# First mixer of a decoder trunk: reversed value rows through DRAM, and a head's diagonal blocks masked in one operation

## Chip, cores and metric

The kernel runs on one core of a Trainium2 chip. The metric is the device time of one execution in microseconds (us), and the median of several runs is compared. In the text, PE is TensorE (matmuls), DVE is VectorE, ACT is ScalarE, POOL is GpSimd and SP is SyncE, which here only issues transfers.

## What is computed

Two consecutive layers of a decoder, on 256 tokens of width 2048 in fp32. Layer 0 mixes with a gated MLP over chunks (A) and a gated linear recurrence, HGRN2 (B); layer 1 mixes with forgetting attention; behind each mixer stands a gated MLP with a short convolution. The change concerns mixer B of layer 0 alone. Cut to what matters:

```python
def hgrn2(q, f_logit, i, g, lower_bound, o_gain):     # (1, 256, 8 heads x 128)
    log_f = logaddexp(log(lb), log1p(-lb) + log_sigmoid(fl))
    k = (1.0 - lb) * sigmoid(-fl)
    ...
    def step(state, xs):                               # chunks of 64 tokens
        G = cumsum(lf_c, axis=2)
        o_inter = einsum('bhtk,bhkv->bhtv', q_c * exp(G), state)
        decay = exp(where(mask[:, :, None], G_t - G_s, -inf))
        scores = einsum('bhtk,bhtsk,bhsk->bhts', q_c, decay, k_c)
        o_intra = einsum('bhts,bhsv->bhtv', scores, v_c)
        ...
    o = rms_norm(o, o_gain) * silu(g)

def mixer_ab(h, ...):
    u, v, q, f, i, g = split(h @ w_in, cuts, axis=-1)   # i are the values of B
    ...
    return concatenate([y_a, hgrn2(q, f, i, g, ...)], axis=-1) @ w_out
```

## The kernel before

**Projections.** The weights stream from DRAM in pieces of 128 x 1024 floats. SP issues the loads, ACT makes the high half of each piece (`wh`, L182), DVE the low half (`wl`, L183), and PE multiplies three times: high by high, high by low, low by high. Three pairs of `wh` and `wl` are kept in the first mixer. `project` gives one head's columns of the query (L301, 24 matmuls for a piece), `project_four` four blocks at a time (L344 to L346), and `project_tok` rows by tokens (L325 to L327), which is what the values use.

**Order of the work.** The tiles and the semaphores are made by a framework that orders each engine's instructions when the program is built: by the place in the program, and by when their operands are expected to be ready. The author steers it by generators. `tick()` is called once for each piece of weights and moves each generator in flight on to its next `yield`; `depth` says how many may be in flight; `held` puts an instruction behind the latest `wh` or `wl`, and `tied` puts a matmul behind the latest matmul of the projection. `start` runs a generator up to its first `yield` at once.

**The heads.** `hgrn(h)` is one generator per head, for eight heads, each begun at least four ticks (`PACE`) after the one before. The 256 tokens of a head lie as two halves of 128, and the second half (T = 1) is kept in reverse order. Step by step:

1. Factors: ACT and DVE make `lf` and `kd` (L695, L699), POOL multiplies (L701 to L709).
2. Diagonal blocks: 16 small matmuls (L714, 32 x 32 each) into a PSUM bank `dg`; four DVE operations (L717) multiply the blocks by the mask `two` into the head's square `st`.
3. Levels: products for spans of 1 to 64 tokens; DVE multiplies factors into `kq` (L722, L733, L736), ACT copies pieces to `E` (L729).
4. Five ticks later, matmuls of the levels (L743, L751) go to a bank `xps` and two tiles of PSUM kept for the purpose, `within[0]` (four levels) and `within[1]` (the level of one token's span, columns 0 to 127). ACT copies from `xps` (L754, L756), and DVE copies five levels into `st` under a mask (L762, `copy_predicated`); ACT then reverses a half to `s1` (L765).
5. Five or six ticks later, and not before the values of its four heads are there (`itoks`), the head's output: L773 to L775, then ACT (L777, L781).

**The values.** `values(j)` runs ahead of the query projections of heads 4 and 7 and makes the values of four heads each. The second half must have its rows reversed. For this `project_tok` is given a place `room`, and POOL copies each piece of the activations in reversed order (`ar`, L316), so that the products of T = 1 come out reversed. The factors of the rows (`Rt`) are reversed too, once, by `mirror` (seven small DVE operations, L616 to L621), to `Rr`. Two ACT operations (L798) take the products from PSUM to `itok`.

The order of the stages in the first mixer is: values of A, forget gates, queries of heads 0 to 3, values 0, queries 4 to 6, values 1, query 7, gates of B, `u` of A, output projection.

Of the kernel before, what the change touches and what calls it, by code (L numbers as in the profile page):

```python
# [8 lines left out]
F32 = mybir.dt.float32  # L9
F32R = mybir.dt.float32r  # L10
U16 = mybir.dt.uint16
AF = mybir.ActivationFunctionType
ALU = mybir.AluOpType
AX = mybir.AxisListType

P = 128
S = 256
# [7 lines left out]
BLK = 32  # L25
# [8 lines left out]
LANE = 64  # L34
SMALL = 4
LEVELS = (64, 32, 16, 8, 4, 2, 1)
NL = len(LEVELS)
# [17 lines left out]
def tile_trunk(ctx: ExitStack, tc: tile.TileContext, x, pp_d, cst_d, mlev_d, msk_d,  # L55
               w_v, w_f, w_g, w_i, w_q, w_u, w_abo, w_cf, w_cqkv, w_cg, w_co, w_up, w_dn, spw_d, spb_d, out):
    nc = tc.nc
    V, SC, PE = nc.vector, nc.scalar, nc.tensor
# [9 lines left out]
    def nm(base):  # L68
        count[0] += 1
        return f"{base}_{count[0]}"  # L70
# [3 lines left out]
    for c0, n in ((0, 1), (1, 1), (2, 2), (4, 2), (6, 2), (8, 4), (12, 4)):  # L74
        t = cp.tile([P, n, S], F32, tag=f"x{c0}", name=f"x{c0}")
# [29 lines left out]
    def view(ap, off, *dims):  # L105
        return bass.AP(ap.tensor, ap.offset + off, [list(ap.ap[0])] + [list(d) for d in dims])
# [12 lines left out]
    def bank():  # L119
        return psum["pool"].tile([P, 512], F32, tag="px", name=nm("px"), bufs=psum["banks"])  # L120
# [21 lines left out]
    def start(g):  # L142

        if next(g, g) is not g:
            flight.append(g)
# [64 lines left out]
    def cols2(ap):  # L210
        return ap.rearrange("p (b c) -> p b c", b=2)
# [4 lines left out]
    def of_two(ps):  # L216
        return view(ps, 0, (1, 2), (2, 256))
# [89 lines left out]
    def project_tok(wsrc, norm, room=None):  # L307

        ps = [pm.tile([P, 512], F32, tag="pm", name=nm("pm")) for _ in range(2)]
        for k in range(0, KT, 2):  # L310
            tick()
            wh, wl = weights(wsrc[:, k * 512:(k + 2) * 512], 1024)
            if room is not None:
                ar = room()
                for i in range(2):
                    nc.gpsimd.tensor_copy(ar[:, i * S:(i + 1) * S].rearrange("p (u n) -> p u n", u=2),  # L316
                                          view(norm.a[k + i], S - 1, (S, 2), (-1, P)))
            for T in range(2):
                for i in range(2):
                    a = norm.a[k + i]  # L320
                    ah, al = a[:, T * P:(T + 1) * P], a[:, S + T * P:S + (T + 1) * P]
                    if T and room is not None:
                        ah, al = ar[:, i * S:i * S + P], ar[:, i * S + P:(i + 1) * S]
                    h, l = (by_two(t, i) for t in (wh, wl))
                    PE.matmul(to_two(ps[T]), ah, h, start=k + i == 0, stop=False)  # L325
                    PE.matmul(to_two(ps[T]), ah, l, start=False, stop=False)  # L326
                    deep["last"] = PE.matmul(to_two(ps[T]), al, h, start=False, stop=k + i == KT - 1)  # L327
        return ps
# [59 lines left out]
    def held(r, last="wh"):  # L388

        tc.add_manual_dep(r.ins, deep[last].ins.name, order, reason="not before")  # L390
# [98 lines left out]
    def mixer_ab(norm):  # L489
        es = ExitStack()  # L490
        hp = es.enter_context(tc.tile_pool(name="hp", bufs=1))
        px = banks(es, 2)
# [18 lines left out]
        for g, ps in enumerate(project_first(w_v, norm, lambda: queue.append(finish()))):  # L511
# [5 lines left out]
            else:  # L517
                drain()
                Rt = norm.Rt
# [20 lines left out]
        two = hp.tile([P, 2, P], F32, tag="pairs", name="pairs")  # L540
# [9 lines left out]
        def tied(r):  # L550
            tc.add_manual_dep(r.ins, deep["last"].ins.name, order, reason="not before")
            return r
# [15 lines left out]
        def mixes():  # L568
            def sums(g, T):
                i = (2 * g + T) * 4  # L570
                j = hp.tile([P, 512], F32, tag="junk", name=nm("junk"), bufs=1)
                held(V.tensor_tensor(j, gv[g][:, T], gv[g][:, T], ALU.mult), "wl")
                V.tensor_reduce(ss[:, i:i + 4], j.rearrange("p (h d) -> p h d", d=P), AX.X, ALU.add)

            halves_ = [(g, T) for g in (1, 0) for T in range(2)]
            for i, (g, T) in enumerate(halves_):
                yield
                held(act(cols2(gv[g][:, T]), of_two(last[T]) if g else cols2(gv[0][:, T]), AF.Gelu,
                         scale=Rt[:, T:T + 1]))
                if i:  # L580
                    sums(*halves_[i - 1])
            yield
            sums(*halves_[-1])
            yield
            tables()
            rsq(ss[:, 0:2 * NH], ss[:, 0:2 * NH], P)
            bound()
            for g in range(2):
                yield
                for T in range(2):  # L590
                    i = (2 * g + T) * 4
                    v4 = gv[g][:, T].rearrange("p (h d) -> p h d", d=P)
                    held(V.tensor_tensor(v4, v4, ss[:, i:i + 4].unsqueeze(2).to_broadcast([P, 4, P]),
                                         ALU.mult), "wl")
            yield
            held(V.tensor_tensor(wt[0], wt[0], tri.unsqueeze(1).to_broadcast([P, NH, P]), ALU.mult), "wl")
            yield
            yield
            for h in range(0, NH, 2):
                ps = bank()  # L600
                both = [mix(h + i, ps[:, i * S:(i + 1) * S]) for i in range(2)]
                for m in both:
                    next(m)
                for m in both:
                    next(m, None)
                yield
            yield from mirror()


        Rr = hp.tile([P, LANE], F32, tag="Rr", name="Rr")[:, 0:2]  # L610

        def mirror():
            yield
            r = hp.tile([P, 512], F32, tag="junk", name=nm("junk"), bufs=1)
            ra, rb = (r[:, i * BLK:(i + 1) * BLK] for i in range(2))
            held(V.tensor_copy(ra, Rt[:, 1:2].to_broadcast([P, BLK])), "wl")  # L616
            V.tensor_copy(Rr[:, 0:1], Rt[:, 0:1])
            V.transpose(rb, ra)
            V.transpose(ra, view(rb, BLK - 1, (-1, BLK)))
            for a in range(4):  # L620
                V.tensor_copy(Rr[BLK * (3 - a):BLK * (4 - a), 1:2], ra[BLK * a:BLK * (a + 1), 0:1])  # L621


        gam = pp[:, C_GAM:C_GAM + 3 * NH]
# [38 lines left out]
        for j in range(2):  # L663
            ps = project_four(w_f[4 * j:4 * j + 4], A, KT)
# [3 lines left out]
            t = hp.tile([P, 1024], F32, tag="o", name=nm("turn"), bufs=2)  # L668
# [5 lines left out]
        itoks, left, os_ = [], [NH], []  # L674
# [5 lines left out]
        for st in sts:  # L680
            V.memset(st, 0.0)

        within = [px.tile([P, 512], F32, tag=f"lv{i}", name=f"lv{i}") for i in range(2)]
        for w in within:
            V.memset(w, 0.0)
        first = [0]
# [1 line left out]
        def hgrn(h):  # L688
# [19 lines left out]
                tot[2 * n] = tots[:, S - 2 * m:S - m]  # L708
                nc.gpsimd.tensor_tensor(tot[2 * n], view(tot[n], 0, (2, m)), view(tot[n], 1, (2, m)), ALU.mult)  # L709
            yield  # L710
            dg = bank()
            for T in range(2):
                for r in range(0, P, BLK):
                    tied(PE.matmul(dg[r:r + BLK, T * BLK:(T + 1) * BLK], kd[:, T, r:r + BLK], t[:, 2 - T, r:r + BLK],  # L714
                                   start=True, stop=True))
            for r in range(0, P, BLK):
                V.tensor_tensor(st[r:r + BLK, :, r:r + BLK], dg[r:r + BLK, 0:2 * BLK].rearrange("p (a b) -> p a b", a=2),  # L717
                                two[r:r + BLK, :, r:r + BLK], ALU.mult)
            yield

            qs = view(t, 2 * P, (1 - P, 2), (2, H))
# [32 lines left out]
            SC.activation(back(s128), xps[:, 0:P], AF.Copy)  # L754
            for r in (0, H):
                SC.activation(st[r:r + H, r // H, H - r:P - r], xps[r:r + H, P:P + H], AF.Copy)  # L756
            for li in reversed(range(1, NL - 1)):

                n = LEVELS[li]
                d, c = places[li]  # L760
                sv = view(st[:, 1], 0, (2 * n, 64 // n), (n - P, 2), (1, n))
                V.copy_predicated(sv, *(t_.rearrange("p (b two n) -> p b two n", two=2, n=n)  # L762
                                        for t_ in (msk[:, li * P:(li + 1) * P], d[:, c:c + P])))
# [27 lines left out]

        gz = []

        def values(j):
            ps = project_tok(w_i[j], norm, lambda: hp.tile([P, 512], F32R, tag="ar", name=nm("ar"), bufs=3))
            itok = hp.tile([P, 2, 512], F32, tag="tok", name=nm("itok"), bufs=2)
            for T in range(2):
                SC.activation(cols2(itok[:, T]), of_two(ps[T]), AF.Copy, scale=Rr[:, T:T + 1])  # L798
            itoks.append((itok, steps[0]))

        silu = []

        def gated(j):
            while left[0] > NH - 4 * (j + 1):
# [23 lines left out]

        for h in range(NH):
            if h in (4, 7):  # L830
                values(len(itoks))
            while len(kq) <= h:
                tick()
            if h % 4 == 0:
                os_.append(hp.tile([P, 2, 512], F32, tag="o", name=nm("o"), bufs=2))
            ps = project(w_q[h], A)
            for T in range(2):
                q = kq[h][:, 2 - T]
                SC.activation(back(q) if T else q, view(ps, T, (2, P)), AF.Copy, scale=omlb[:, h:h + 1])
            queue.append(hgrn(h))  # L840
# [591 lines left out]
```

## Time and profile before

| what | before |
|---|---|
| median of 3 runs | 2175.03 us (2174.26 to 2176.19) |
| the profiled execution | 2173.92 us |
| its span | 2172.1 us |
| granted TensorE clock | 1.00 |
| busy: PE, DVE, ACT, POOL | 2164.0, 1601.1, 1313.6, 472.3 us |
| matmuls | 10874 |
| DMA traffic | 483.55 MB, mean 223 GB/s |

The span is the time from the first to the last instruction of the profiled execution. "Busy" adds up the time in which an engine executes; matmuls overlap each other, and their ends are modelled. The rows of groups give the line of the kernel, the engine, the operation, output and input by the program's names, the shapes, the count, then busy time in us, the mean duration in ns, and the idle time of the engine before these instructions with what ended it. The rows of waits give the total in us, how often, and the longest. The rows of a timeline begin with the start and the length in us.

### The profile page before, as it was taken

How to read it: one execution, taken by the hardware profiler on the slowest of the kernel's cores; microseconds unless marked ns; L12 is line 12 of the kernel's file. 1: busy time of each engine (PE TensorE's matmuls, PEld its weight loads, DVE VectorE, ACT ScalarE, POOL GpSimd, SP SyncE). 2: the span in 40 equal slices, each digit the busy share in tenths (PEclk: the TensorE clock that was granted, in tenths of full speed). 3: DMA queues.
4: the chain of work that ended last, by engine and by line, in shares of the span. 5: the costliest groups of instructions: out<-in, count | busy, mean ns of one | idle time of the engine just before them, and what ended most of it. 6: DMA issues, size and time to landing. Idle time of an engine off the chain costs nothing.

```text
span 2172.1 us, 32509 instructions
## 1 busy us (share of the span) xinstructions
PE 2164.0 (100%) x10874; PEld 1900.8 (88%) x10874; DVE 1601.1 (74%) x2286; ACT 1313.6 (60%) x1951; POOL 472.3 (22%) x865
## 2 busy tenths in 40 slices
PE   9999999999999999999999999999999999999999
PEld 8988888888888888888888888888888888888888
DVE  7788768777567757776987887877777577667766
ACT  7678766665556545654666556666666466456642
POOL 1252221212012002111233443212211012011202
PEclk9999999999999999999999999999999999999999
DMA  8655677777676767776777766787777677666866
GB/s 311 209 160 177 209 238 222 240 233 236 210 228 206 235 209 219 226 237 206 241 230 229 238 207 209 221 246 222 230 227 242 198 232 217 228 215 204 251 212 192
DMA packets 492617, 483.55 MB, mean 223 GB/s; under 512 B 115137, under 2 KB 460369, under 8 KB 492321
## 3 DMA queue, kind: packets, MB, share of 16 engines
q1 hardware_dynamic: 465888, 453.27, 66.2%
q0 software_dynamic: 24832, 25.92, 5.1%
q10 hardware_dynamic: 1728, 2.28, 0.3%
q8 instruction: 85, 1.39, 0.3%
q14 instruction: 84, 0.68, 0.1%
HBM read 435.18 MB, written 2.11 MB: 201 GB/s over the span
## 4 chain that ended last, share of the span: by engine, by line
PE 94%; DVE 2%; ACT 2%; issue 1%; DMA 1%; POOL 0%; SPq 0%; ACTq 0%; DVEq 0%
PE pm L344 26%; PE pm L345 26%; PE pm L346 26%; PE pm L325 4%; PE pm L326 4%; PE pm L327 4%; PE pm L233 1%; PE pm L301 1%; ACT wh L182 1%; DVE wl L183 1%; DMA pt<-ptmp 1%; PE pm L257 1%; DVE kq L733 0%; ACT E L729 0%; DVE st L762 0%
## 5 line engine op out<-in xcount | busy, mean ns | idle before, releaser
L183 DVE TENSOR_TENSOR wl<-w,wh 128x1024 fp32r<-128x1024 f32 (+1 forms) x820 | 990.9, 1218 | 448.7 <-ACT wh L182 437.0
L182 ACT ACTIVATE wh<-w 128x1024 fp32r<-128x1024 f32 (+1 forms) x820 | 856.0, 1049 | 608.8 <-PE pm L346 447.7
L344 PE MATMUL pm<-wh,a 128*128 128x512 f32 x1728 | 655.9, 380 | 0.0
L345 PE MATMUL pm<-wl,a 128*128 128x512 f32 x1728 | 655.3, 379 | 0.3 <-DVE wl L183 0.3
L346 PE MATMUL pm<-wh,a 128*128 128x512 f32 x1728 | 654.9, 379 | 0.0
L364 POOL DMA_DIRECT2D zt<-tmp x413 | 223.5, 549 | 1134.6 <-DVE tmp L357 1022.6
L345 PEld LDWEIGHTS pm<-wl,a 128*128 128x128 f32 x1728 | 326.6, 189 | 47.4 <-DVE wl L183 1.4
L346 PEld LDWEIGHTS pm<-wh,a 128*128 128x128 f32 x1728 | 326.6, 189 | 46.2
L344 PEld LDWEIGHTS pm<-wh,a 128*128 128x128 f32 x1728 | 326.5, 189 | 46.2
L344 PE MATMUL pm<-wh,hid 128*128 128x512 f32 x688 | 260.8, 379 | 0.0
L345 PE MATMUL pm<-wl,hid 128*128 128x512 f32 x688 | 260.8, 379 | 0.0
L346 PE MATMUL pm<-wh,hid 128*128 128x512 f32 x688 | 260.8, 379 | 0.0
L326 PE MATMUL pm<-wl,a 128*128 128x512 f32 x416 | 158.1, 380 | 2.3 <-DVE wl L183 2.3
L325 PE MATMUL pm<-wh,a 128*128 128x512 f32 x416 | 158.7, 381 | 0.0
L327 PE MATMUL pm<-wh,a 128*128 128x512 f32 x416 | 157.8, 379 | 0.0
L345 PEld LDWEIGHTS pm<-wl,hid 128*128 128x128 f32 x688 | 130.0, 189 | 18.5
L346 PEld LDWEIGHTS pm<-wh,hid 128*128 128x128 f32 x688 | 130.0, 189 | 18.5
L344 PEld LDWEIGHTS pm<-wh,hid 128*128 128x128 f32 x688 | 130.0, 189 | 18.4
L1238 ACT ACTIVATE conv<-zt,pp 128x256 f32<-128x256 f32 x176 | 95.9, 590 | 70.6 <-DMA zt<-tmp 62.5
L364 POOL DMA_DIRECT2D turn<-tmp x160 | 86.9, 551 | 224.4 <-DVE tmp L357 129.6
L1239 DVE SCALAR_TENSOR_TENSOR conv<-zt,pp,conv 128x255 f32<-128x255 f32 x176 | 80.2, 479 | 54.4 <-ACT conv L1238 35.4
L357 DVE STREAM_TRANSPOSE tmp<-z 128x512 f32<-128x512 f32 x120 | 97.8, 851 | 7.1 <-ACT z L1224 5.1
(252 smaller groups left out, 2245.2 us busy)
## 6 DMA issues: line engine op xcount, KB each, us to landing
w<-in_w_up SPq DMA_DIRECT2D x352, 512.0 KB, 5.0
w<-in_w_dn SPq DMA_DIRECT2D x176, 512.0 KB, 5.0
w<-in_w_cqkv SPq DMA_DIRECT2D x96, 512.0 KB, 4.6
w<-in_w_abo SPq DMA_DIRECT2D x32, 512.0 KB, 4.9
w<-in_w_cg SPq DMA_DIRECT2D x32, 512.0 KB, 5.3
w<-in_w_co SPq DMA_DIRECT2D x32, 512.0 KB, 4.9
zt<-tmp SPq DMA_DIRECT2D x414, 32.0 KB, 2.6
zt<-tmp POOLq DMA_DIRECT2D x413, 32.0 KB, 2.4
```

Of the source, the lines that this page charges most:

```text
L182: r = deep["wh"] = SC.activation(wh, w, AF.Copy)
L183: deep["wl"] = V.tensor_tensor(wl, w, wh.bitcast(F32), ALU.subtract)
L325: PE.matmul(to_two(ps[T]), ah, h, start=k + i == 0, stop=False)
L326: PE.matmul(to_two(ps[T]), ah, l, start=False, stop=False)
L327: deep["last"] = PE.matmul(to_two(ps[T]), al, h, start=False, stop=k + i == KT - 1)
L344: PE.matmul(to_rows(ps[T]), ah, h, start=not begun and k + i == ks[0], stop=False)
L345: PE.matmul(to_rows(ps[T]), ah, l, start=False, stop=False)
L346: deep["mm"] = deep["last"] = PE.matmul(to_rows(ps[T]), al, h, start=False, stop=not more and k + i == ks[-1] + 1)
L357: V.transpose(tmp.rearrange("p (b m i t) -> p b m i t", b=4, m=4, t=2)[:, :, :, :, T], src(T).rearrange("p (m b j) -> p b m j", m=4, b=4))
L364: queues[(a + b) % len(queues)].dma_start(dst[BLK * b:BLK * (b + 1), :, a * n:(a + 1) * n], tmp[BLK * a:BLK * (a + 1), b * 4 * n:(b + 1) * ...
L1238: held(SC.activation(c, z, AF.Identity, bias=pp[:, cb:cb + 1], scale=w(2)))
L1239: V.scalar_tensor_tensor(c[:, 1:], z[:, :S - 1], w(1), c[:, 1:], ALU.mult, ALU.add)
```

## The change

The values: `project_tok` is called without `room`, so POOL copies nothing, and the products of T = 1 come out in normal order. ACT takes them to a tile `late`, with the unreversed factors `Rt`. A new generator `flip` then moves `late` to DRAM, from there to DRAM with the rows reversed, and from there to `itok[:, 1]`: three transfers of 256 KB, all issued on ACT's queue, with a tick between them. The values are entered in `itoks` with the third, two ticks later than before. `mirror` and `Rr` go.

The diagonal blocks: the 16 matmuls write into columns 128 to 383 of `within[1]`, each block in its own place in two 128 x 128 fields, which were set to zero once. One DVE operation multiplies the whole field by `two` into the whole of `st`. The bank `dg` is no longer taken. In the level copies, level 1 (a span of 32) moves from the last place to the first.

```diff
-            yield from mirror()
-
-        Rr = hp.tile([P, LANE], F32, tag="Rr", name="Rr")[:, 0:2]
-
-        def mirror():
...
-        within = [px.tile([P, 512], F32, tag=f"lv{i}", name=f"lv{i}") for i in range(2)]
+        within = [px.tile([P, n], F32, tag=f"lv{i}", name=f"lv{i}") for i, n in enumerate((512, 512))]
...
-            dg = bank()
+            dg = within[1][:, P:3 * P].rearrange("p (a b) -> p a b", a=2)
             for T in range(2):
                 for r in range(0, P, BLK):
-                    tied(PE.matmul(dg[r:r + BLK, T * BLK:(T + 1) * BLK], kd[:, T, r:r + BLK], t[:, 2 - T, r:r + BLK],
+                    tied(PE.matmul(dg[r:r + BLK, T, r:r + BLK], kd[:, T, r:r + BLK], t[:, 2 - T, r:r + BLK],
                                    start=True, stop=True))
-            for r in range(0, P, BLK):
-                V.tensor_tensor(st[r:r + BLK, :, r:r + BLK], dg[r:r + BLK, 0:2 * BLK].rearrange("p (a b) -> p a b", a=2),
-                                two[r:r + BLK, :, r:r + BLK], ALU.mult)
+            V.tensor_tensor(st, dg, two, ALU.mult)
...
-            for li in reversed(range(1, NL - 1)):
+            for li in (1, *reversed(range(2, NL - 1))):
...
+        def flip(itok, late, r, f):
+            SC.dma_start(r, late)
+            yield
+            SC.dma_start(bass.AP(f.tensor, f.offset, [[S, 2], [512, P], [1, S]]),
+                         bass.AP(r.tensor, r.offset + (P - 1) * 512, [[S, 2], [-512, P], [1, S]]))
+            yield
+            SC.dma_start(itok[:, 1], f)
+            itoks.append((itok, steps[0]))
+
         def values(j):
-            ps = project_tok(w_i[j], norm, lambda: hp.tile([P, 512], F32R, tag="ar", name=nm("ar"), bufs=3))
+            ps = project_tok(w_i[j], norm)
             itok = hp.tile([P, 2, 512], F32, tag="tok", name=nm("itok"), bufs=2)
-            for T in range(2):
-                SC.activation(cols2(itok[:, T]), of_two(ps[T]), AF.Copy, scale=Rr[:, T:T + 1])
-            itoks.append((itok, steps[0]))
+            late = hp.tile([P, 512], F32, tag="ar", name=nm("late"), bufs=1)
+            SC.activation(cols2(late), of_two(ps[1]), AF.Copy, scale=Rt[:, 1:2])
+            SC.activation(cols2(itok[:, 0]), of_two(ps[0]), AF.Copy, scale=Rt[:, 0:1])
+            start(flip(itok, late, *rowsd[j]))
...
+        dp = es.enter_context(tc.tile_pool(name="da", bufs=1, space=bass.MemoryType.DRAM))
+        rowsd = [[dp.tile([P, 512], F32, tag=f"rd{i}{n}", name=f"rd{i}{n}") for n in range(2)] for i in range(2)]
...
-                values(len(itoks))
+                values(h // 7)
```

More of the change, by code (lines that the diff above doesn't have):

```diff
@@ L606, in mixes @@
                 yield
-            yield from mirror()
-        Rr = hp.tile([P, LANE], F32, tag="Rr", name="Rr")[:, 0:2]
-        def mirror():
[L613 to L621, printed above, removed]
         gam = pp[:, C_GAM:C_GAM + 3 * NH]
```

## Prediction

> **What bounds the kernel now.** I read the page first.
>
> ```profile
> span 2172.1 us, 32509 instructions
> PE 2164.0 (100%) x10874; PEld 1900.8 (88%) x10874; DVE 1601.1 (74%) x2286; ACT 1313.6 (60%) x1951; POOL 472.3 (22%) x865
> ```
>
> TensorE (PE) is busy for 2164.0 of 2172.1 us, and the change adds and removes no matmul: 16 block products per head stay 16 products, and a projection with reversed stationary rows stays a projection. So the time can fall only by PE's idle time. The second view is the waits of PE alone:
>
> ```profile
> PE pm L326 <- DVE wl L183: 2.3, 3, 1.3
> PE warm L149 <- DVE ones L85: 1.1, 1, 1.1
> PE pm L301 <- DVE wl L183: 0.6, 1, 0.6
> PE pm L345 <- DVE wl L183: 0.3, 1, 0.3
> ```
>
> These are all that PE waits for in the whole span, 4.3 us; the warm-up's 1.1 is out of reach, so 3.2 us remain. All three of them wait for `wl`, the low half of a weight piece that VectorE (DVE) makes. L326 is the token projection that the values use. The third view, stretches of 10 us (sum, then busy time and count of PE, weight loads, DVE, ACT and POOL; clock, DMA share, GB/s), shows that the waits lie where the change is made:
>
> ```profile
> 122.00:132.00 10.00, 9.92 (x107) 8.33 (x105) 8.52 (x19) 6.31 (x18) 7.70 (x13) 1.00 0.59 189
> 132.00:142.00 10.00, 8.38 (x105) 7.21 (x106) 8.61 (x13) 7.24 (x19) 9.64 (x15) 1.00 0.51 157
> 182.00:192.00 10.00, 9.42 (x116) 8.75 (x115) 8.08 (x18) 8.47 (x27) 0.94 (x3) 1.00 0.43 135
> ```
>
> The clock is 1.00. PE drops to 8.38 of 10 where DVE is at 8.61 and GpSimd (POOL) at 9.64. Fourth, the chain of waits between 128 and 140 us (start, length, what):
>
> ```profile
> 130.27 0.23 DVE st L717
> 130.53 0.45 DVE st L762
> 132.05 1.11 DVE wl L183
> 135.09 1.34 DVE wl L183
> 136.47 0.48 PE pm L326
> ```
>
> Here the path runs over DVE: the masks of a head's diagonal blocks (L717), the copies of its levels (L762), then the `wl` for which PE waits. DVE work taken out of this place can come back as PE time, up to the 3.2 us.
>
> **Part 1: one mask operation for four.** DVE in the stage of the heads (out<-in, count, busy, mean ns, idle):
>
> ```profile
> L183 DVE TENSOR_TENSOR wl<-w,wh 128x1024 fp32r<-128x1024 f32 x25 | 31.4, 1258 | 4.3 <-ACT wh L182 4.2
> L733 DVE TENSOR_TENSOR kq<-kq,tot 128x256 f32<-128x256 f32 x31 | 16.1, 519 | 7.5 <-ACT E L729 7.5
> L717 DVE TENSOR_TENSOR st<-px,pairs 32x64 f32<-32x64 f32 x24 | 5.3, 221 | 0.4
> ```
>
> Four masks cost 4 x 0.221 = 0.884 us a head. The new one is 128x256 with one operand in PSUM, a form that the trace doesn't have. Above: 0.519, the same shape at L733. Below: 1.258 / 4 = 0.31 from L183, which does four times the columns. I take 0.45, nearer to L733. Saved: 0.43 us a head, 3.5 us in eight heads (2.9 to 4.6), all on DVE and none of it directly on PE.
>
> **Part 2: no POOL copies.** 32 casts of 128x256 go:
>
> ```profile
> L316 POOL CAST ar<-a x32: 395/586/1447, 5.6 to 178.0; 128x256 fp32r<-128x256 f32 x32
> 124.44 4.49 POOL L316 CAST ar<-a 128x256 fp32r<-128x256 f32 x6
> 126.03 1.41 DVE L183 TENSOR_TENSOR wl<-w,wh 128x1024 fp32r<-128x1024 f32 x1
> 127.37 0.61 DVE L733 TENSOR_TENSOR kq<-kq,tot 128x256 f32<-128x256 f32 x1
> 178.63 1.23 DVE L183 TENSOR_TENSOR wl<-w,wh 128x1024 fp32r<-128x1024 f32 x1 [0.31 <-ACT wh L182]
> 179.78 0.42 DVE L733 TENSOR_TENSOR kq<-kq,tot 128x256 f32<-128x256 f32 x1
> ```
>
> PE waited for none of the casts, so their own time is hidden behind PE's work. But six of them stand from 124.44 to 128.93, and the DVE operations inside that stretch took 1.41 and 0.61 us where the same operations took 1.23 and 0.42 without them: 0.2 us each. With some three such operations under the casts before each of the waits, that is 0.6 us of DVE for the first values stage and about as much for the second. [...]
>
> Reversing the rows' factors (`mirror`) goes too:
>
> ```profile
> L621 DVE COPY Rr<-junk 32x1 f32<-32x1 f32 x4 | 0.6, 145 | 0.1
> ```
>
> Seven operations of about that size, some 1 us of DVE (seven by 145 ns), all before the heads begin, where PE has no wait in the list. Worth nothing.
>
> Together: of the three waits on `wl`, 2.9 us fall in the values stages or at their end. The longest is 1.3 us, with one mask right ahead of it and casts shortly before. I let 2.0 of the 3.2 us go (0 to 3.2). What is late next is the ScalarE (ACT) cast `wh`, ahead of each `wl` (the 4.2 us of idle in the L183 row).
>
> **Part 3: the diagonal products get another place.** Before, they went to a bank of their own; now they go to columns 128 to 383 of the PSUM tile whose columns 0 to 127 hold the last level of an earlier head. The order in time at present:
>
> ```profile
> 125.51 0.53 PE L751 MATMUL lv<-E 128*32 128x32 f32 x38
> 125.99 0.33 PE L714 MATMUL px<-kq,kd 128*32 128x32 f32 x16
> 129.93 0.43 ACT L756 ACTIVATE st<-px 64x64 f32<-64x64 f32 x2
> 130.53 0.45 DVE L762 COPY_PREDICATED st<-msk,lv 128x128 f32<-128x128 uint16 x1
> 131.02 0.30 DVE L762 COPY_PREDICATED st<-msk,lv 128x128 f32<-128x128 uint16 x1
> 141.73 0.51 ACT L729 ACTIVATE E<-kq 128x128 f32<-128x128 f32 x2
> 151.62 0.39 PE L743 MATMUL px<-kq 128*128 128x128 f32 x2
> ```
>
> Head 0's levels (L751) are followed at once by head 2's diagonal products (L714, 0.33 us for 16), and DVE copies head 0's levels only 4.5 us later. The new list of levels puts level 1 first, so the copy out of the shared tile is the second, ending at 131.3. If the products must wait for it, they stand 131.3 - 126.0 = 5.3 us later; behind them are VectorE's `kq` product (L722), which overwrites what they read, and that head's twelve copies to `E` (L729). The last of these ends at 142.2, and PE takes up that head's levels only at 151.6 (L743), so 5 us there are covered by the 9.4 us between. What isn't covered is PE itself, which takes its instructions in order. Price per head, for the six heads that have a predecessor by two: 0 if the build puts other matmuls ahead of the products, 5.3 us if it doesn't. That it orders by expected readiness is seen in this trace: the first casts of L316 run at 5.6 us, though they belong to the values stage. What is left is its error of expectation, whose nearest row is PE's own longest wait on DVE, 1.3 us, in a list where most pieces have none. I take 0.25 us a head, +1.5 us in all, and keep 0 to 5.3.
>
> [...]
>
> **Part 4: the second half of the values goes through DRAM.** Out by one transfer, reversed by a second, in by a third, each waiting for the one before, all issued on ACT's queue, in two stages. Rows for the cost (KB and us to landing; the ACT queue's issue in ns):
>
> ```profile
> w<-in_w_i SPq DMA_DIRECT2D x16, 512.0 KB, 3.6
> turn<-tmp SPq DMA_DIRECT2D x8, 32.0 KB, 2.5
> L524 ACTq DMA_DIRECT2D kst<-in_msk x1: 659/659/659, 40.8 to 40.8; - x1
> DMA to landing us min/median/max: 3.1/6.2/8.2
> ```
>
> A transfer of 256 KB lies between 2.5 and 8.2 us, nearest to the 3.6 of a 512 KB piece in the same stage; three make 7.5 to 24.6, taken as 10.8. When the values are needed:
>
> ```profile
> 140.32 1.26 ACT L798 ACTIVATE itok<-pm,Rr 128x512 f32<-128x512 f32 x2
> 145.59 0.39 PE L773 MATMUL px<-itok,st 128*128 128x128 f32 x2
> 185.24 5.40 PE pm L301 x46
> 186.65 0.67 ACT L798 ACTIVATE itok<-pm,Rr 128x512 f32<-128x512 f32 x1
> 196.72 0.38 PE L773 MATMUL px<-itok,st 128*128 128x128 f32 x2
> ```
>
> Head 0's output (L773) begins 4.0 us after the values are in SBUF; the code moves it on by one piece of weights, 24 matmuls, 24/46 x 5.40 = 2.8 us. At 10.8 us the values come 10.8 - 6.8 = 4.0 us after that place. Head 4's output has 9.4 us: 1.4 late. Again PE loses this only where it reaches the product too early; the third transfer is known to the build as a long step, so other matmuls can stand ahead. I take a quarter of 5.4 us, rounded down: +1.0 us (0 to 5.4).
>
> On ACT each stage gains three issues of 0.33 to 0.66 us and two waits for a landing. Queued behind such a wait are the `wh` casts of the next pieces, and DVE and PE behind those. ACT works 6.3 to 8.5 of 10 us in this stage, so six issues, 2 to 4 us, mostly fit into its idle time: +0.5 us (0 to 3).
>
> **Sum.** On the profiled execution (2173.92 us for a span of 2172.1): -2.0 + 1.5 + 1.0 + 0.5 = +1.0, so 2174.9. The median of the runs, 2175.03, lies 1.1 higher: 2176.0 us. About 0.2%, 4.35 us, is what a measurement of this kernel can tell from no change, so this counts as no change.
>
> **The rivals.**
>
> *PE waits at the diagonal products.* One mechanism: the products sit in PE's order right behind the levels or too soon after, and wait for DVE's second level copy. For it: they stand next to each other now, and DVE is 4.5 us behind at that place. Against it: the order is made by expected readiness, and a PE that waits lets `wl` catch up, which takes back the 3.2 us. At half the 5.3 us, six heads cost 15.9, less 3.2: +12.7, 2187.7; at 1.3 us each, 7.8 - 3.2 + 1.5 for part 4: +6, 2181. It decides from about (4.35 + 2.0 - 1.5) / 6 = 0.8 us a head on.
>
> *The values come late.* Three landings at the 6.2 us of the other ACT transfers make 18.6 us: 11.8 late at head 0 and 9.2 at head 4. If PE bears half of that, +10.5, and with the mixed gains of part 1 and 2 gone in it +8.5: 2183.5. Against it: weight pieces of twice the size land in 3.6 us in this stage.
>
> *All the gains and none of the costs.* -3.2: 2171.8. That is 0.15%, still within 0.2%. To be faster by more, PE would have to lose stalls that the list of waits doesn't show. A change without any effect, because PE is the bound everywhere, would give 2175.0 and counts the same way.
>
> **How the numbers follow.** Forecast with its neighbours, from 2171.5 to 2179: 0.62. Diagonal products: 0.20, from 2179.4 up to some 2204. Late values: 0.12, from 2179.4 to 2186. Faster by over 0.2%: 0.06. The likeliest case is the forecast, 2176.0. The range begins at 2171.5, the full gain, and runs to 2187, which leaves out 0.06 below and about 0.1 of the upper part of the first rival. Chances: faster 0.06, same 0.62, slower 0.32.
>
> **What would show it.** Right: L316 gone; one mask a head of 0.31 to 0.52 us; the waits of PE on `wl` in the first mixer under 1.5 us in all; new PE waits below 0.8 us each at the diagonal products and at the output products; the three landings of a stage near 10.8 us. Wrong: PE waiting over 1 us a head for L762, or for a landing ahead of L773; `wh` casts held behind ACT's transfer issues, with `wl` waits larger than now; a PE busy sum that changes, which the argument excludes.

## The result: 0.9% slower, and the profile after

| kernel | median us | ratio to before, 95% interval |
|---|---|---|
| before | 2175.03 | 1 |
| changed | 2194.96 (2192.55 to 2196.11, 5 runs) | 1.0089 [1.0074, 1.0103] |

The forecast was 2176.0 with a range up to 2187.0; the change costs 19.9 us. The profiled execution has a span of 2193.3 us, 21.2 more than before. First the head of the page and PE's waits (total, times, longest):

```profile
span 2193.3 us, 32457 instructions
PE 2170.8 (99%) x10874; PEld 1904.3 (87%) x10874; DVE 1594.5 (73%) x2254; ACT 1314.5 (60%) x1951; POOL 448.9 (20%) x833
PE pm L344 <- ACT wh L182: 6.7, 1, 6.7
PE px L758 <- DMA itok<-rd: 5.2, 1, 5.2
PE lv L699 <- POOL tot L694: 1.9, 2, 1.3
PE pm L345 <- DVE wl L183: 1.1, 2, 0.7
PE pm L301 <- DVE wl L183: 0.9, 2, 0.5
PE lv L699 <- DVE st L745: 0.7, 2, 0.5
```

The number of matmuls is the same. Two single waits make 11.9 us: one of a matmul for its weights' high half `wh`, one of the first head's output (L758 is the old L775) for the values. The waits for `wl`, 3.2 us before, are 2.0 now. L699 are the diagonal products, a new place. Then the stretches around the two large waits (sum, then busy time and count of PE, weight loads, DVE, ACT, POOL; clock, DMA share, GB/s):

```profile
152.00:157.00 5.00, 0.00 (x0) 0.00 (x0) 0.78 (x1) 2.08 (x5) 1.02 (x2) 0.84 0.48 167
157.00:162.00 5.00, 4.83 (x66) 4.60 (x66) 2.52 (x5) 3.19 (x12) 0.00 (x0) 0.50 0.60 178
204.00:211.00 7.00, 0.52 (x3) 0.12 (x1) 1.55 (x4) 1.64 (x3) 0.66 (x2) 0.69 0.17 61
211.00:217.00 6.00, 5.72 (x14) 4.13 (x15) 4.11 (x7) 3.83 (x6) 4.87 (x7) 0.51 0.51 157
217.00:222.00 5.00, 5.00 (x42) 4.35 (x41) 2.84 (x6) 4.08 (x11) 0.00 (x0) 1.00 0.63 197
```

The third number from the end of a row is the granted clock. It falls already inside the idle stretch; after it PE works for 5 to 6 us at 0.50 and 0.51 of full speed, and only then at 1.00. Narrower stretches show 1.00 up to 155.3 us, 0.50 from 155.4 to 162.2 and 1.00 from 162.3; in the second stage 1.00 up to 206.5, 0.50 from 206.6 to 216.8 and 1.00 from 216.9. In the second stage's chain of waits most matmuls stand with 0.43 us each up to 216.7, and with 0.22 behind it. At half speed 5.0 us lose 2.5, and 6.0 lose 2.9, an estimate from these rows. The longest wait before, 1.3 us, left the clock at 1.00. Runs below show a lower clock behind shorter waits than 5.2 and 6.7 us: `diag_four` a mean of 0.58 over 4 us behind a wait of 2.8 us, and `cols8`, whose longest wait is 3.4 us, 0.69 from 203 to 208 us, behind a stretch of 5 us in which PE was busy for 1.11.

What ACT does in the meantime (start, length; "ACTq" are transfers that it issues; in brackets its idle time before the instruction, and what ended it):

```profile
140.48 0.34 ACTq L778 DMA_DIRECT2D rd<-late  x1
145.84 1.21 ACTq L780 DMA_DIRECT2D rd<-rd  x1
154.55 0.33 ACTq L783 DMA_DIRECT2D itok<-rd  x1
154.92 0.32 ACT L685 ACTIVATE kd<-kq 128x128 f32<-128x128 f32 x1 [5.05 <-DMA rd<-rd]
155.14 1.04 ACT L182 ACTIVATE wh<-w 128x1024 fp32r<-128x1024 f32 x1
208.97 0.32 ACTq L783 DMA_DIRECT2D itok<-rd  x1
209.34 0.22 ACT L739 ACTIVATE st<-px 64x64 f32<-64x64 f32 x1 [6.32 <-DMA rd<-rd]
210.09 1.99 ACT L182 ACTIVATE wh<-w 128x1024 fp32r<-128x1024 f32 x2
```

ACT stands for 5.05 and 6.32 us at the issue of the third transfer (L783), until the second has landed; the `wh` casts that PE needs come right behind. At the issue of the second (L780) it stands 2.0 us more in the second stage, until the first has landed. The chain of waits gives the landings of the first stage, 16.6 us together:

```profile
140.48 5.33 DMA rd<-late
145.84 8.69 DMA rd<-rd
154.55 2.58 DMA itok<-rd
```

In the first stage two things are late at once. PE stands for the values from 151.95 to 157.17; of pieces of weights it had some 2 us of work left there (an estimate: 14 matmuls of the query and the levels, which took 4.1 us at half clock after the wait), and the next `wh` was made only from 155.14.

So of the 21.2 us, 11.9 are the two waits, 5.4 the half clock by the estimate above, 2.8 the waits at L699 (one more wait, of 0.2 us for L719, counted with the rows shown), and the other waits roughly cancel those gone. Some 1 us is not assigned.

### The profile page after: what moved, and what is told of

Same layout as the page of the kernel before. It is cut to its first block, busy times and chain, and to the rows that moved or that the text cites. A ratio compares the mean times of both kernels' runs of the same rounds, so it can differ in the third digit from the quotient of the medians.

```text
span 2193.3 us, 32457 instructions
## 1 busy us (share of the span) xinstructions
PE 2170.8 (99%) x10874; PEld 1904.3 (87%) x10874; DVE 1594.5 (73%) x2254; ACT 1314.5 (60%) x1951; POOL 448.9 (20%) x833
## 3 DMA queue, kind: packets, MB, share of 16 engines
q8 instruction: 85, 1.39, 0.3%
## 4 chain that ended last, share of the span: by engine, by line
PE 87%; DMA 3%; ACT 1%; DVE 1%; issue 1%; SPq 1%; POOL 0%; ACTq 0%; DVEq 0%
PE pm L345 25%; PE pm L346 25%; PE pm L344 25%; PE pm L327 4%; PE pm L325 4%; PE pm L326 4%; DMA rd<-rd 1%; SPq L364 1%; ACT wh L182 1%; DMA pt<-ptmp 1%; DMA rd<-late 0%; DVE wl L183 0%; PE pm L301 0%; DVE tmp L357 0%; PE px L1021 0%
## 5 line engine op out<-in xcount | busy, mean ns | idle before, releaser
L344 PE MATMUL pm<-wh,a 128*128 128x512 f32 x1728 | 656.9, 380 | 6.7 <-ACT wh L182 6.7
L345 PE MATMUL pm<-wl,a 128*128 128x512 f32 x1728 | 656.5, 380 | 1.2 <-DVE wl L183 1.1
L346 PE MATMUL pm<-wh,a 128*128 128x512 f32 x1728 | 655.9, 380 | 0.0
L325 PE MATMUL pm<-wh,a 128*128 128x512 f32 x448 | 170.8, 381 | 0.6 <-ACT a L382 0.6
L327 PE MATMUL pm<-wh,a 128*128 128x512 f32 x448 | 170.2, 380 | 0.0
L326 PE MATMUL pm<-wl,a 128*128 128x512 f32 x448 | 169.8, 379 | 0.0
```

The lines of the kernel that those rows point to most:

```text
L344: PE.matmul(to_rows(ps[T]), ah, h, start=not begun and k + i == ks[0], stop=False)
L345: PE.matmul(to_rows(ps[T]), ah, l, start=False, stop=False)
L346: deep["mm"] = deep["last"] = PE.matmul(to_rows(ps[T]), al, h, start=False, stop=not more and k + i == ks[-1] + 1)
```

## The experiments

Two theories. Theory 1: the time is lost to the chain of transfers. Theory 2, the first rival of the prediction: PE waits at the diagonal products, which now lie in a shared PSUM tile.

**The halves of the change.** `values_only` is the changed kernel with `dg`, the four masks and the order of the levels as before; `diag_only` is the kernel before with

```diff
-            dg = bank()
+            dg = within[1][:, P:3 * P].rearrange("p (a b) -> p a b", a=2)
...
+            V.tensor_tensor(st, dg, two, ALU.mult)
...
-            for li in reversed(range(1, NL - 1)):
+            for li in (1, *reversed(range(2, NL - 1))):
```

> The values' half of the change alone; the diagonal blocks keep their own bank and four masks. Theory 1 (the time is lost to the chain of three transfers): PE waits about 5 us for the values at the first head's output, is idle again about 7 us when ACT stands at the third transfer of the second stage, and runs at half clock for some 5 us after each; +16 to +20 us over before. Theory 2 (the diagonal products in the shared PSUM tile hold PE): within 3 us of before.

> The diagonal blocks' half of the change alone (shared PSUM tile, one mask operation, level 1 first); the values stay as before, with the GpSimd copies. Theory 1: -3 to +2 us against before, PE's waits at the diagonal products below 0.8 us each. Theory 2: +10 to +17 us, PE waiting over 1 us a head for the level copies.

Measured: `values_only` 2195.49 us, 1.0089 [1.0074, 1.0104], the whole loss; `diag_only` 2178.15 us, 1.0009 [0.9999, 1.0018]. PE's waits of the first and then of the second:

```profile
PE pm L344 <- ACT wh L182: 9.0, 1, 9.0
PE px L760 <- DMA itok<-rd: 5.6, 1, 5.6
```

```profile
PE lv L714 <- DVE st L760: 3.2, 4, 1.6
PE pm L345 <- DVE wl L183: 2.1, 3, 0.8
PE lv L714 <- POOL tot L709: 0.6, 1, 0.6
```

Theory 2 falls as the cause. Its wait exists: L714, the diagonal products, waits for the level copies (`st` L760) 0.3 to 1.6 us at a time, so not always below the expected 0.8. The build put in this wait between columns 128 to 383 and the copy out of columns 0 to 127; what the chip would do without it no run here shows.

**The middle transfer.** `cols8` writes it as eight column parts:

```diff
-            SC.dma_start(bass.AP(f.tensor, f.offset, [[S, 2], [512, P], [1, S]]),
-                         bass.AP(r.tensor, r.offset + (P - 1) * 512, [[S, 2], [-512, P], [1, S]]))
+            SC.dma_start(bass.AP(f.tensor, f.offset, [[64, 8], [512, P], [1, 64]]),
+                         bass.AP(r.tensor, r.offset + (P - 1) * 512, [[64, 8], [-512, P], [1, 64]]))
```

> The changed kernel with the middle transfer (DRAM to DRAM) written as eight column parts of 64 and not two of 256. Its 256 packets of 1 KB ran one after the other at about 25 ns, as if on two engines, and took 8.5 to 8.7 us to land. If the first size of the pattern sets how many engines share it, the transfer lands in about 4 us, the chain in 12, and most of PE's idle time goes: +2 to +9 us over before. If it is the latency of DRAM or the number of packets, it lands in 8 us or more and the time is +18 us or more.

Measured: 2186.89 us, 1.0056 [1.0039, 1.0073]. The chain of its first stage:

```profile
138.84 6.02 DMA rd<-late
144.88 4.34 DMA rd<-rd
149.24 2.66 DMA itok<-rd
```

The middle transfer lands in 4.34 us where it took 8.69 (in the second stage 4.91 and 8.46), with four times as many rows in its pattern, of 256 bytes in place of 1 KB, and 8 us of the loss go. The time is 11.0 us over before, so the landing came as expected and the gain (+2 to +9) did not. In the changed kernel the transfer's 256 packets of 1 KB run for 6.4 us of the landing (147.8 to 154.2), with two of them at a time on average: 11.9% of 16 engines, 1.9, for their queue in this stretch. The other 2.3 us lie before and behind them. If these stay, some 2.0 us are left for the packets of `cols8`, an estimate from the two landings; the whole is then halved and not quartered. The first size of the pattern, which the expectation names, fits the two landings; but the length of the rows changed with it, and which of the two does it is not shown.

**Another queue.** In `pool_queue` the three `SC.dma_start` of `flip` become `nc.gpsimd.dma_start`.

> The changed kernel with its three transfers a stage issued on GpSimd's queue in place of ACT's. Theory 1 in two parts: ACT is free, so the second stage's idle time of PE (6.8 us) and the half clock after it (about 3 us) go, while the first head still waits for its values: +6 to +11 us over before. If PE's second idle time came from the values themselves and not from ACT standing in its queue, it stays, and the time is as after, +18 to +22.

Measured: 2201.59 us, 1.0119 [1.0104, 1.0135], against the expectation. The two large waits of PE in the heads' stage are gone, but a new one stands from 292.2 to 299.2 us:

```profile
PE pm L344 <- ACT yb L396: 7.1, 1, 7.1
L783 POOL DMA_DIRECT2D itok<-rd x2: 601/605/609, 185.3 to 220.7; - x2
L758 PE MATMUL px<-itok,s x16: 273/275/275, 195.8 to 283.0; 128*128 128x128 f32 x16
```

The build put the third transfer of the first stage behind POOL's work for the heads, at 185.3 us in place of 154.6. The heads' outputs run from 195.8 to 283.0, where they ran from 157.2 to 255.6, and the output projection waits for what follows from them. This run leaves open what ACT's standing costs; it shows that heads which come late for 30 us are paid for at the end of the mixer.

**ACT's standing by itself.** `unread` is the kernel before with the three transfers added on ACT's queue, to a tile that nobody reads:

```diff
+            late = hp.tile([P, 512], F32, tag="ar", name=nm("late"), bufs=3)
+            start(flip(itok, late, *rowsd[j]))
```

Here `flip` sends `itok[:, 1]` out, and its third transfer comes in to `late`.

> The kernel before, with the same three transfers a stage added on ACT's queue: the finished second half of the values goes out, is reversed and comes in to a tile that nobody reads. No head waits for them; only ACT stands in its queue for their landings. If ACT's standing is worth the second idle time by itself: PE idle 5 to 9 us in the second stage behind a missing high half, at half clock afterwards, and +7 to +13 us over before in all. If it is the late values that count in both stages: +0 to +2 us.

Measured: 2197.43 us, 1.0098 [1.0083, 1.0113], more than expected and as much as the whole change. PE's waits, and ACT's idle time that the second landing ended:

```profile
PE pm L344 <- ACT wh L182: 8.8, 1, 8.8
PE pm L301 <- ACT wh L182: 8.7, 1, 8.7
ACT st L756 <- DMA rd<-rd: 6.4, 1, 6.4
ACT px L781 <- DMA rd<-rd: 5.1, 1, 5.1
```

No head waits for a value here. ACT stands 5.1 and 6.4 us, the same as in the changed kernel, and PE lacks `wh` in both stages. That ACT stands is enough for the loss. PE's waits are longer than ACT's stops; the first stage shows why:

```profile
157.36 0.37 ACT L781 ACTIVATE px<-o,Rt 128x128 f32<-128x128 f32 x1 [5.14 <-DMA rd<-rd]
158.17 1.04 ACT L182 ACTIVATE wh<-w 128x1024 fp32r<-128x1024 f32 x1
159.26 0.79 PE L301 MATMUL pm<-a,wh 128*128 128x256 f32 x2 [8.73 <-ACT wh L182]
```

PE was out of `wh` from 150.5, before ACT stopped at 152.2, and when ACT goes on, it first works off what stands ahead of the cast (0.8 us), and then casts for 1.0 us.

**More time between the transfers.** `paced` puts 2 and 3 ticks between them, `cols8_paced` 2 and 2 with the eight column parts:

```diff
             SC.dma_start(r, late)
-            yield
+            for _ in range(2):
+                yield
...
-            yield
+            for _ in range(3):
+                yield
             SC.dma_start(itok[:, 1], f)
```

> The changed kernel with the second and third transfer of a stage put 2 and 3 ticks after the one before (before: 1 and 1), and so the values entered 3 ticks later; transfers and queue as in the changed kernel. A tick is some 2.7 us, the landings 5.3 and 8.7 us, so ACT should reach each issue about when its transfer has landed. If the loss is issues that come before the landing and a head that comes before its values: both idle times of PE and both stretches at half clock go, within -2 to +4 us of before. If later heads then hold up the gates of B, PE waits near 250 us and the time is +5 or more.

> The changed kernel with the middle transfer in eight column parts (4.4 to 4.9 us to landing) and both transfers 2 ticks after the one before. Chain of about 13 us against 4 ticks of 2.7 and a landing of 2.7: nothing should wait. -3 to +2 us against before; -2 if the GpSimd copies and masks that are saved come back as PE time, 0 if they do not.

Measured: 2187.89 us, 1.0054 [1.0040, 1.0068], and 2181.30 us, 1.0025 [1.0015, 1.0035]: 12.0 and 5.4 us over before. Both miss what was expected (up to +4 and +2): better than without the ticks, but not level. ACT's waits in `paced` from 130 to 215 us:

```profile
ACT lf L680 <- DMA rd<-rd: 6.5, 1, 6.5
ACT wh L182 <- DMA rd<-rd: 5.0, 1, 5.0
ACT sos L99 <- DMA rd<-late: 1.4, 1, 1.4
```

ACT stands as long as in the changed kernel, 6.5 and 5.0 us. In spite of the later place in the program the issues still come before the landing in ACT's order. PE's loss is smaller (one wait of 2.9 us at the longest). In the first stage the first head's output now stands at 161.7 us, so PE waits for no values; in the second a `wh` cast (at 194.2 us) lies between the second issue and the third, where the changed kernel has none.

**SP's queue.** `sp_queue` and `cols8_sp` issue the transfers with `nc.sync.dma_start`, the latter with the eight column parts; all else is the changed kernel.

> The changed kernel with its transfers issued on SP's queue, which otherwise issues only the weight loads, ahead of their use. ACT stands for nothing. If ACT's standing alone makes the loss (theory 1 as the run with unread transfers has it), what is left is the wait for late values at the first head, about 5 us and the half clock behind it: +4 to +9 us over before. If the late values matter nothing either: -2 to +3. If SP's standing delays the weights just as much: +15 or more.

> As the one before, with the middle transfer in eight column parts. The chain is some 13 us in place of 16.6 and SP stands half as long: -1 to +4 us against before, at least 3 us less than with two column parts if late values are what is left there.

Measured: 2176.60 us, 1.0007 [0.9998, 1.0016], and 2177.43 us, 1.0006 [0.9997, 1.0015]. PE's waits and the transfers of `sp_queue`:

```profile
PE pm L345 <- DVE wl L183: 1.2, 2, 1.0
PE lv L699 <- DVE st L745: 0.8, 2, 0.4
143.83 0.70 SPq L780 DMA_DIRECT2D rd<-rd  x1
146.28 2.71 SPq L195 DMA_DIRECT2D w<-in_w_i  x2
151.80 0.33 SPq L783 DMA_DIRECT2D itok<-rd  x1
L758 PE MATMUL px<-itok,s x16: 272/275/275, 166.0 to 236.9; 128*128 128x128 f32 x16
```

The same transfers with the same dependences cost nothing measurable here. The values land some 2 us earlier than in the changed kernel (third issue at 151.80, 3.1 to 3.6 us to landing, where it was 157.1), but still 3 us after the place where PE stood for them there (151.95). Yet no PE wait for them is left: the build put the first product that reads them at 166.0, not 157.2, with other matmuls ahead. What values that come too late for PE's order cost by themselves is therefore not separated; what is shown is that with ACT free the loss is gone, and that the shorter middle transfer is worth nothing once ACT does not wait for it.

**What the rest can bring.** `no_flip` makes the values without copies, mirrored factors or transfers (here against the changed kernel):

```diff
+            for T in range(2):
+                SC.activation(cols2(itok[:, T]), of_two(ps[T]), AF.Copy, scale=Rt[:, T:T + 1])
+            itoks.append((itok, steps[0]))
```

> Leaves the reversal of the values out altogether: the second half goes to its place in normal order, so part of the output differs. No GpSimd copies, no mirrored factors, no transfers; the diagonal blocks as before. It gives what the removal of the copies can be worth at most: -3.2 us if PE's waits on the low halves come from DVE operations slowed by the copies, 0 if they do not.

Measured: 2174.35 us, 0.9994 [0.9985, 1.0003]; PE still waits 1.8 us in the token projection:

```profile
PE pm L326 <- DVE wl L183: 1.8, 3, 1.0
```

It is 1.2 us ahead of before, an amount that these runs don't tell from nothing.

`diag_old_order` is `diag_only` with `for li in reversed(range(1, NL - 1))`, and `diag_four` is that with the four masks:

```diff
-            V.tensor_tensor(st, dg, two, ALU.mult)
+            for r in range(0, P, BLK):
+                V.tensor_tensor(st[r:r + BLK, :, r:r + BLK], dg[r:r + BLK, :, r:r + BLK],
+                                two[r:r + BLK, :, r:r + BLK], ALU.mult)
```

> The diagonal blocks' half alone, with the levels copied in the old order, so that the copy out of the shared PSUM tile is the first of five and not the second. If PE's waits at the diagonal products (4 waits, 3.2 us in the run with the new order) are for this copy, they shrink by one copy each, to about 2 us, and the time is 1 us less than that run's, level with before within 1 us. If they are not, they stay at 3 us.

> The diagonal products in the shared PSUM tile, levels in the old order, but masked in four operations as before. Against the same kernel with one mask operation (2177.9 us, 2.0 over before): if the one operation's saved 0.47 us a head on DVE comes back as PE time, this one is 1 to 3 us slower; if the DVE time is hidden, it is level within 1 us, and the 2 us over before are the shared tile's.

Measured: 2177.86 us, 1.0010 [1.0001, 1.0019], level with `diag_only`, with waits that did not shrink; and 2181.40 us, 1.0029 [1.0019, 1.0039]. In this order:

```profile
PE lv L714 <- DVE st L760: 4.3, 5, 1.6
```

```profile
PE lv L714 <- DVE st L762: 5.4, 4, 2.8
132.00:136.00 4.00, 4.00 (x12) 3.19 (x13) 3.86 (x11) 2.09 (x5) 2.17 (x7) 0.58 0.36 125
```

The order of the levels does not set the wait's length: the miss of the first expectation. The wait is for the copy out of the shared tile all the same (it holds the level of a span of two tokens, `LEVELS[5]`). At the longest wait the products follow 0.48 us after DVE's copies begin in the old order, where that copy is the first, and 0.82 us in the new order, where it is the second; what is long is the time until DVE comes to the copies. With the shared tile given, the single mask is worth some 3.5 us; part of that is a mean clock of 0.58 for the 4 us after one longer wait of `diag_four`, not DVE time as such. Against the four masks with a bank of their own, the kernel before, nothing is gained.

No experiment points to a version that beats the kernel before: the reversal for nothing is worth 1.2 us within its uncertainty, and the diagonal half costs about 2.

## Why the prediction was wrong, point by point

**The bound: right.** PE's work did not change, and the cap on the gain (3.2 us of waits for `wl`) held: `no_flip` stays inside it.

**Part 1, the mask: right in size, without a gain.** The new operation:

```profile
L701 DVE TENSOR_TENSOR st<-lv,pairs x8: 417/418/425, 104.9 to 218.1; 128x256 f32<-128x256 f32 x8
```

0.418 us, taken as 0.45. The saved DVE time, 0.47 us a head, does not show as PE time against the kernel before: `diag_only` and `diag_old_order`, which have it, are some 2 us slower.

**Part 2, the copies: the gain of 2.0 us, meant for parts 1 and 2 together, was too large.** The removal of the copies alone (`no_flip`) measured 1.2 us, with an interval that reaches past zero, and the mask showed no gain. The waits for `wl` in the token projection, 2.3 us before, are 1.8 without any copy. One reading of the rows was short: in the trace before, a cast next to a `wl` (1.28 and 1.41 us) took 1.39 us and ended 0.26 us after it, where a cast without a DVE operation beside it took 0.40. So it was mostly GpSimd's cast that took longer, by about 1 us, and DVE's operation lost the 0.2. (`mirror` is eight operations, not seven; this changes nothing.)

**Part 3, the diagonal products: about right.** +1.5 us was predicted for waits beside a gain in DVE time; the half alone came out at +2 us, with four or five waits for the copies of 0.8 us on average (0.3 to 1.6). The rival of 1.3 to 2.7 us a head was not the case.

**Part 4: the step that failed, twice.** First, the landings: 10.8 us for three, measured 16.6. The nearest row, a 512 KB piece in 3.6 us, was a bad neighbour for the middle transfer, which took 8.69 us with a pattern whose first size is 2 (and 4.34 with one of 8, in `cols8`). With that, the late values, taken as +1.0 us, cost one wait of 5.2 us at head 0, the upper end of their range. Second, and this carries the loss: "six issues, 2 to 4 us, mostly fit into its idle time: +0.5 us (0 to 3)". The working named the `wh` casts behind ACT's waits, also as a sign of being wrong, and then priced only the issues. A wait for a landing is not work that fills idle time; here it held everything behind it on ACT. ACT stood 5.1 and 6.3 us, PE ran out of `wh` (6.7 us in one wait of the second stage; in the first the wait for the values lay over it), and the half clock after each idle stretch, which the prediction does not have at all, added 5.4 us by the estimate above.

**The rivals.** The late values had 0.12 and a price of 2183.5. Place and transfers were right, and its landings of 6.2 us each (18.6 in all) were near the 16.6. Its mechanism was there once: PE waited 5.2 us for the values at head 0's output, about half of the 9.8 us by which 16.6 exceeds the prediction's allowance of 6.8. But head 4's output waited for nothing, the larger wait was for `wh`, and `unread` loses 21.5 us with no late value; so it names a part of the loss and misses what is enough for the whole. The first rival, with the higher chance, moved the same way for a reason that the runs exclude as the cause.

## What to carry to other kernels

When a chain of dependent transfers is issued by an engine that also computes, price each wait in it by the landing of the transfer before, borne by all that is queued behind (here landings of 8.69 and 8.46 us, for which ACT stood 5.1 and 6.3); put such a chain on a queue whose engine is ahead of its use (on SP's the kernel took 2176.60 us, on ACT's 2194.96). The price of a hidden engine's stop is not its length: 5.1 us became a wait of 8.7 in `unread`, and in `paced`, where ACT stood 6.5 us, PE's longest wait was 2.9. Count how much of what PE needs lies ahead of the stop, and what has to be worked off behind it; and where PE runs dry, look at the clock behind it: after waits of 5.2 and 6.7 us it stood at 0.50 and 0.51, after one of 2.8 at 0.58, after one of 1.3 at 1.00. Of a transfer look at the pattern before taking a duration from another of like size: the same 256 KB took 8.69 us with a first size of 2 and rows of 1 KB, and 4.34 with 8 and 256 bytes.

## What the runs showed of the hardware that was not expected

The clock at 0.50 for 5 to 6 us after PE's idle times of 5.2 and 6.7 us, and its mean of 0.58 over 4 us in `diag_four` after one of 2.8. A DRAM-to-DRAM transfer of 256 KB at 8.69 us in two parts and 4.34 us in eight, with rows of 256 bytes in place of 1 KB. And an ordering of the build that, given the same dependences on POOL's queue, issued the third transfer 31 us later and lost more than it saved.
